# A retention layer whose first two heads take their values by seven products of halves, in turns with queries and keys

## The chip, the core and the metric

The kernel runs on one core of one Trainium2 chip. The metric is the device time of one execution in microseconds (us), the median over runs. Five engines work side by side and meet through semaphores: TensorE (PE in the profile, its weight loads PEld), VectorE (DVE), ScalarE (ACT), GpSimd (POOL) and SyncE (SP), which here only issues DMAs. POOL issues DMAs too: those that add what they bring to what lies in the buffer (accumulate DMAs).

## The reference

Two pre-norm layers on x of 512 tokens by 1024, float32. Layer 0 mixes tokens with a chunked gating MLP, layer 1 with retention; each is followed by a dense MLP with squared ReLU, and a last RMSNorm closes. The change lies in the retention:

```
proj = xn @ w_in                       # xn = rmsnorm(x, g), 1024 wide
q, k, v, g = split(proj)               # 4 heads: q, k 256 wide each; v, g 512 wide each
q = rotary(q, cos, sin); k = rotary(k * dk**-0.5, cos, sin)
o = decayed causal attention of q, k, v   # the kernel: (q k^T * decay) v over all 512 tokens
o = rmsnorm(o per head, head_norm_g) * silu(g)
return o @ w_out
```

## The kernel before

All products are made of 128x512 matmuls on TensorE. Float32 is kept up by splitting every operand in a high part (a rounded copy, made by ACT for weights, `wH`) and a low part (the rest, a subtraction on DVE, `wL`). `mm3` (the matmuls of L265) then issues three matmuls for each product: high by high, high by low, low by high. A piece of weights is 128x1024 or so, and a projection of 1024 inputs to 128 outputs over all tokens is one piece and 24 matmuls; this is one unit of TensorE's work here.

The order of the whole program is written as a list of steps. Each step (`step`) is given its weight pieces. A step issues its matmuls, then `advance` (continues generators that were left pending: second halves of evacuations), then `refill`, which issues the high splits of pieces up to three ahead (`LOOK = 3`) and the low splits up to two ahead, and, when a buffer comes free, the next weight load on SP's queue; then what was hung behind the step. The engines run their own lists in just this order, so what an engine has behind a waiting instruction waits too. Weights land in two buffers of 1 MB of their own (`raw`), and in a third where a stage gives one (`extra`). A generic pool, `bigp`, gives blocks of 1 MB. PSUM has six accumulators (`acc`) and two banks for small things (`mis`).

A layer's norm is applied late: hH and hL hold x times the gain, split, and the factor of each token (`r4` by partition, `rbc` spread over a row) is multiplied in after the product. In retention it goes into the cosines and sines (`trig_scaled`, L869), into the evacuation of v (L906, L907) and of g. The norm's sum of squares is reduced over partitions by two matmuls (`st_mix`, L320, L321) and spread by two (`bc_mix`, L339, L340).

`rope` (L876 to L886) takes the two halves of a head's q or k: four multiplications on DVE, one subtraction and one addition on POOL, then, at the next `advance`, two ACT casts and two DVE subtractions. `scores` makes q k^T by decay, `av` the product with v, `evac_g` the gate, `head_norm` and `make_y` the norm of a head and its split, `o_unit` the output projection. The order is: v of head 0, q and k of head 0, g of head 0 with its scores, q and k of head 1 with `av` of head 0, v of head 1 with its scores and the norm of head 0, g of head 1 with its `av`, output of head 0; then for heads 2 and 3 q and k, v with scores, g with `av`, and the output of the head before.

The dense MLP already uses seven products of halves (Strassen) for its second weight matrix, three times a layer: `seven` (L710 on) splits a product of 512x1024 by 1024x1024 in 256-token, 512-input and 512-output halves. The sums of weights are made by accumulate DMAs on POOL's queue (L200), the sums of activations by `make` (L732 to L755), whose pieces are called `sp`, and the seven products in banks a, b and c are added into `ytok` by ACT (first one, L785) and DVE (L787). There the fourteen pieces of the products take turns with `up` projections.

Of the kernel before, what the change touches and what calls it, by code (L numbers as in the profile page):

```python
# [17 lines left out]
P = 128  # L18
T = 512
# [67 lines left out]
def trunk(ctx, tc, x, norm_mix_g, norm_ffn_g, a_w_in, a_b_in, a_v_norm_g, a_w_s, a_b_s, a_w_out,  # L87
# [6 lines left out]
    bigp = ctx.enter_context(tc.tile_pool(name="bigp", bufs=16))  # L94
# [14 lines left out]

    def z2t(name):  # L110
        return tmp(name, "z2", 4)
# [598 lines left out]
    def seven(l, q):  # L710

        w = mlp_w2[l]

        def part(i, j):
            r, c = 1024 * q + 512 * i, 512 * j
            return w[r : r + 512, c : c + 512].rearrange("(k p) n -> p k n", p=P)
# [6 lines left out]
        lo_t, hi_t = slice(0, T // 2), slice(T // 2, T)  # L723
        sums, parts, banks = {}, {}, {}

        def block(h, ts, c):
            return aF[2 * q + h][:, 2 * c : 2 * c + 2, ts]

        def half(v):
            return v.rearrange("p (k t) -> p k t", t=T // 2)  # L730

        def make(s):  # L732

            def src(c):
                if s in (0, 2, 6):
                    return block(*((0, lo_t), None, (1, lo_t), None, None, None, (1, hi_t))[s], c)
                if s == 1:
                    sums["s", c] = half(tmp(f"sa{l}{q}{c}", "uz"))
                    nc.vector.tensor_sub(out=sums["s", c], in0=block(0, hi_t, c), in1=block(1, hi_t, c))
                elif s == 3:  # L740
                    nc.vector.tensor_sub(out=sums["s", c], in0=sums["s", c], in1=block(0, lo_t, c))
                elif s == 4:
                    nc.vector.tensor_add(out=sums["s", c], in0=sums["s", c], in1=block(1, lo_t, c))
                else:
                    sums["d", c] = half(tmp(f"sd{l}{q}{c}", "sq"))
                    nc.vector.tensor_sub(out=sums["d", c], in0=block(0, lo_t, c), in1=block(0, hi_t, c))
                    return sums["d", c]
                return sums["s", c]

            sp = parts[s] = big([P, 2, 4, T // 2], F32R, f"sp{l}{q}{s}")  # L750
            for c in range(2):
                v = src(c)
                hi, lo = sp[:, 0, 2 * c : 2 * c + 2, :], sp[:, 1, 2 * c : 2 * c + 2, :]
                nc.scalar.copy(out=hi, in_=v)
                nc.vector.tensor_sub(out=lo, in0=v, in1=f32(hi))  # L755
# [5 lines left out]
        PLAN = (0, 1, 2, 3, 5, 4, 6) if q == 2 else range(7)  # L761
# [28 lines left out]

        return (lambda: make(0)), [lambda s=s: [step(one(s, i), pl[s][i]) for i in range(2)] for s in PLAN]

    fresh = set()

    def dense(l, hooks):
# [6 lines left out]
        for q in range(3):  # L802
            pl = pieces_f(mlp_w1[l], (0, D), (1024 * (q + 1), 1024 * (q + 2)))
            first, products = seven(l, q)
# [26 lines left out]
    def down_last(gcol):  # L831
# [14 lines left out]
        for i in range(2, 8):  # L846
            feat(pl[i], last_acts, evac(i), f"dn0_{i}", lambda i=i: back(i))

# [314 lines left out]
```

## Time and profile before

| | |
|---|---|
| time, median of 3 runs | 1373.2 us (1373.09 to 1373.71) |
| the profiled execution's own time | 1372.55 us |
| its span (first to last instruction) | 1370.8 us |
| mean granted TensorE clock | 0.998 |
| PE busy | 1360.1 us (99% of the span) |
| DVE, ACT, POOL busy | 806.8 us (59%), 539.8 us (39%), 164.1 us (12%) |
| retention layer, from its first matmul to its last | 625.55 us to about 1025 us |
| chain of work that ended last | PE 95% |

A row of a group reads: line, engine, operation, output and inputs with their shape, count, then busy time in us, mean duration of one in ns, and the idle time of the engine before them with what ended it. A row of the timeline or of the chain in order of time begins with the start and the duration in us. A row of the table of windows has the length, then each engine's busy time and instruction count, the granted clock, the share of the DMA engines and GB/s.

### The profile page before, as it was taken

What the parts mean: (1) busy time and instruction counts of PE and PEld (TensorE: products, weight loads), DVE (VectorE), ACT (ScalarE), POOL (GpSimd) and SP (SyncE); (2) the same over time, 40 slices, a digit from 0 to 9 for tenths busy, and PEclk for the clock granted to TensorE, in tenths of its full rate; (3) what the DMA queues carried; (4) which work ended last, traced back from release to release, by engine and by line L of the source; (5) the groups of instructions that cost most, each with busy time, mean ns of one, the idle gap of its engine ahead of it and who ended that gap; (6) DMA issues with size and microseconds to landing.
All of it is one profiled execution on the core that took longest, in us unless ns stands there. A gap on an engine that the chain in (4) does not pass through costs nothing.

```text
span 1370.8 us, 15222 instructions
## 1 busy us (share of the span) xinstructions
PE 1360.1 (99%) x6184; PEld 1130.9 (82%) x6184; DVE 806.8 (59%) x1007; ACT 539.8 (39%) x765; POOL 164.1 (12%) x130
## 2 busy tenths in 40 slices
PE   9999999999999999999999999999999999999997
PEld 7888888888888888888888888888888888888886
DVE  7434555675666756775645474365494665665653
ACT  4543423234544434422333432333333543444342
POOL 4001111130100000021112110100121000100002
PEclk9999999999999999999999999999999999999999
DMA  6332222245674848322212222132127375674621
GB/s 234 126 103 92 74 88 87 91 131 154 154 207 126 212 126 183 126 101 95 92 62 75 79 93 93 62 114 71 62 93 212 92 187 159 156 206 127 172 87 61
DMA packets 115798, 166.69 MB, mean 122 GB/s; under 512 B 2880, under 2 KB 67984, under 8 KB 115472
## 3 DMA queue, kind: packets, MB, share of 16 engines
q1 hardware_dynamic: 102448, 139.50, 31.0%
q0 software_dynamic: 12672, 25.17, 10.9%
q8 instruction: 48, 0.79, 0.2%
q10 hardware_dynamic: 608, 1.06, 0.2%
q14 instruction: 22, 0.18, 0.0%
HBM read 163.62 MB, written 2.10 MB: 121 GB/s over the span
## 4 chain that ended last, share of the span: by engine, by line
PE 95%; DVE 2%; DMA 1%; ACT 1%; issue 1%; POOL 0%; SPq 0%; POOLq 0%; ACTq 0%; DVEq 0%
PE up L265 24%; PE g L265 6%; PE ro L265 6%; PE vv L265 6%; PE qk L265 6%; PE u L265 6%; PE o L265 6%; PE v L265 4%; PE dt L265 3%; PE dn L265 2%; PE av L265 2%; PE sm11a L265 2%; PE sm10a L265 2%; PE sm01a L265 2%; PE sm00a L265 2%; PE sm02a L265 2%
## 5 line engine op out<-in xcount | busy, mean ns | idle before, releaser
L228 DVE TENSOR_TENSOR wL<-raw,wH 128x1024 fp32r<-128x1024 f32 x235 | 301.7, 1289 | 63.5 <-PE v L265 18.3
L221 ACT CAST wH<-raw 128x1024 fp32r<-128x1024 f32 x235 | 244.0, 1046 | 86.1 <-PE v L265 15.0
L265 PE MATMUL up<-hH,wH 128*128 128x512 f32 x480 | 187.2, 390 | 0.2 <-ACT xtok L1032 0.2
L265 PE MATMUL up<-hL,wH 128*128 128x512 f32 x480 | 186.8, 389 | 0.0
L265 PE MATMUL up<-hH,wL 128*128 128x512 f32 x480 | 186.8, 389 | 0.0
L687 ACT ACTIVATE aF<-r 128x512 f32<-128x512 f32 x54 | 34.2, 633 | 218.0 <-DVE r L686 218.0
L686 DVE SCALAR_TENSOR_TENSOR r<-up,wide 128x512 f32<-128x512 f32 x54 | 37.4, 692 | 126.5 <-PE up L265 120.1
L265 PEld LDWEIGHTS up<-hH,wH 128*128 128x128 f32 x480 | 90.1, 188 | 19.2 <-ACT xtok L1032 0.5
L265 PEld LDWEIGHTS up<-hH,wL 128*128 128x128 f32 x480 | 90.1, 188 | 18.8
L265 PEld LDWEIGHTS up<-hL,wH 128*128 128x128 f32 x480 | 90.1, 188 | 18.7
L200 POOL DMA_DIRECT2D raw<-in_mlp_w_dram x22 | 28.5, 1297 | 390.4 <-DVE wL L228 244.7
L294 POOL TENSOR_TENSOR ssq<-ssq,sq 128x512 f32<-128x512 f32 x28 | 43.9, 1568 | 151.8 <-ACT sq L293 151.5
L228 DVE TENSOR_TENSOR wL<-more,wH 128x1024 fp32r<-128x1024 f32 x40 | 48.8, 1219 | 5.8 <-issue 4.3
L265 PE MATMUL u<-hH,wH 128*128 128x512 f32 x128 | 50.6, 395 | 0.0
L265 PE MATMUL g<-hH,wH 128*128 128x512 f32 x128 | 50.5, 395 | 0.0
L265 PE MATMUL o<-yH,wH 128*128 128x512 f32 x128 | 50.4, 394 | 0.0
L265 PE MATMUL qk<-hH,wH 128*128 128x512 f32 x128 | 50.0, 391 | 0.0
L265 PE MATMUL vv<-wH,hH 128*128 128x512 f32 x128 | 50.0, 391 | 0.0
L265 PE MATMUL ro<-ryH,wH 128*128 128x512 f32 x128 | 50.0, 390 | 0.0
L265 PE MATMUL ro<-ryH,wL 128*128 128x512 f32 x128 | 50.0, 390 | 0.0
L265 PE MATMUL ro<-ryL,wH 128*128 128x512 f32 x128 | 49.9, 390 | 0.0
L265 PE MATMUL vv<-wL,hH 128*128 128x512 f32 x128 | 49.9, 390 | 0.0
(359 smaller groups left out, 2982.1 us busy)
## 6 DMA issues: line engine op xcount, KB each, us to landing
raw<-in_mlp_w_dram SPq DMA_DIRECT2D x50, 1024.0 KB, 5.1
raw<-in_b_w_in_dram SPq DMA_DIRECT2D x24, 1024.0 KB, 5.0
raw<-in_mlp_w_dram POOLq DMA_DIRECT2D x22, 1024.0 KB, 8.9
more<-in_mlp_w_dram SPq DMA_DIRECT2D x20, 1024.0 KB, 5.2
raw<-in_a_w_in_dram SPq DMA_DIRECT2D x14, 1024.0 KB, 5.2
raw<-in_a_w_out_dram SPq DMA_DIRECT2D x8, 1024.0 KB, 5.0
raw<-in_b_w_out_dram SPq DMA_DIRECT2D x8, 1024.0 KB, 5.0
raw<-in_a_w_in_dram SPq DMA_DIRECT2D x8, 256.0 KB, 6.6
```

The lines of the kernel that those rows point to most:

```text
L200: nc.gpsimd.dma_start(out=r.tile, in_=src, accum_op=ALU.add)
L221: nc.scalar.copy(out=p.hi, in_=p.src)
L228: nc.vector.tensor_sub(out=p.lo, in0=p.src, in1=f32(p.hi))
L265: nc.tensor.matmul(ps, lhsT=a, rhs=b, start=start and i == 0, stop=stop and i == 2, skip_group_check=resumed)
L294: nc.gpsimd.tensor_tensor(out=state["ssq"], in0=state["ssq"], in1=sq, op=ALU.add)
L686: nc.vector.scalar_tensor_tensor(out=r, in0=ps, scalar=0.0, in1=rbc, op0=ALU.max, op1=ALU.mult)
L687: nc.scalar.activation(a, r, AF.Square)
```

## The change

Values of heads 0 and 1 together are a product of 512x1024 by 1024x1024. They are now made by `seven`, as in the dense MLP: seven products of 256-token, 512-input, 512-output halves in place of eight, in the order 0, 1, 2, 3, 5, 4, 6. The activations' side comes from `side_h`: products 0, 2 and 6 use hH and hL as they are, the others use sums built from x times the gain. The results, `vF`, are values without the norm's factor, which is multiplied in when they are split (`split_v`), behind the gates of head 0 and the values of head 2. The pieces of the products take turns with the eight pieces of q and k of heads 0 and 1. The k pieces of these go to the `mis` banks.

With it the order of the layer is rebuilt: after the turns come g of head 0 with its scores, g of head 1 with `av` of head 0, v of head 2 with the scores of head 1 and the norm of head 0, g of head 2 with `av` of head 1, output of head 0, q and k of head 2, output of head 1 with scores of head 2, q and k of head 3 with `av` of head 2, v of head 3, g of head 3, outputs of heads 2 and 3. The evacuation of `av` becomes one DVE instruction for heads 0 to 2. The tables of cosines, sines and decay are loaded at the begin of the layer rather than before the last part of the dense MLP, the decay of two heads at a time; `bigp` has 17 blocks; the third weight buffer of this stage is `morev`; the norm's statistics come after the first product and the first q piece instead of inside v's unit.

```diff
@@ -707,12 +704,12 @@
...
-    def seven(l, q):
-
-        w = mlp_w2[l]
+    def seven(w, row, col, a, dst, name, plan=range(7), behind={}):
...
         def part(i, j):
-            r, c = 1024 * q + 512 * i, 512 * j
+            r, c = row + 512 * i, col + 512 * j
             return w[r : r + 512, c : c + 512].rearrange("(k p) n -> p k n", p=P)
         t1 = Raw(part(0, 0), adds=[part(0, 1)])
...
@@ -720,67 +717,33 @@
...
-            after = dict(zip(PLAN, PLAN[1:])).get(s)
+            then = dict(zip(plan, plan[1:])).get(s)
             def run(p):
                 bk = BANK[s]
                 if i == 0 and s in FIRST:
-                    banks[bk] = [acc(f"sm{l}{q}{bk}{t}") for t in range(2)]
-                sp = parts[s]
+                    banks[bk] = [acc(f"sm{name}{bk}{t}") for t in range(2)]
                 for t in range(2):
-                    ts = slice(t * P, (t + 1) * P)
                     for k in range(2):
                         kk = 2 * i + k
-                        mm3(banks[bk][t], sp[:, 0, kk, ts], sp[:, 1, kk, ts], p.hi[:, k, :], p.lo[:, k, :], s in FIRST and kk == 0, kk == 3, True)
+                        mm3(banks[bk][t], *parts[s](kk, t), p.hi[:, k, :], p.lo[:, k, :], s in FIRST and kk == 0, kk == 3, True)
                 advance()
                 refill()
-                if i == 0 and after is not None:
-                    make(after)
+                if i == 0 and then is not None:
+                    parts[then] = a(then)
+                if (s, i) in behind:
+                    behind[s, i]()
                 if i == 1:
                     (m, n), op = OUT[s]
                     for t in range(2):
-                        v = tok[n][:, 2 * m + t, :]
+                        v = dst[n][:, 2 * m + t, :]
...
@@ -788,7 +751,100 @@
-        return (lambda: make(0)), [lambda s=s: [step(one(s, i), pl[s][i]) for i in range(2)] for s in PLAN]
+        def begin():
+            parts[plan[0]] = a(plan[0])
+        return t1, begin, [lambda s=s: [step(one(s, i), pl[s][i]) for i in range(2)] for s in plan]
...
+    def side_split(sp):
+        return lambda k, t: tuple(sp[:, j, k, t * P : (t + 1) * P] for j in range(2))
...
+    def side_h(gcol, name):
+        sums = {}
+        def g(k):
+            return gT[:, gcol + k : gcol + k + 1]
+        def scaled(c, k0, ts):
+            t = half(sums["all"][:, 2 + c, :])
+            for i in range(2):
+                k = k0 + 2 * c + i
+                nc.scalar.activation(t[:, i, :], xT[k][:, ts], AF.Copy, scale=g(k))
+            return t
+        def combine(out, c, k0, ts, t):
+            for i in range(2):
+                k = k0 + 2 * c + i
+                nc.vector.scalar_tensor_tensor(out=out[:, i, :], in0=xT[k][:, ts], scalar=g(k), in1=t[:, i, :], op0=ALU.mult, op1=ALU.subtract)
+        def make(s):
+            if s in (0, 2, 6):
+                k0, t0 = ((0, 0), None, (4, 0), None, None, None, (4, 2))[s]
+                return lambda k, t: tuple(v[k0 + k][:, (t0 + t) * P : (t0 + t + 1) * P] for v in (hH, hL))
+            sp = big([P, 2, 4, T // 2], F32R, f"sp{name}{s}")
+            for c in range(2):
+                hi, lo = sp[:, 0, 2 * c : 2 * c + 2, :], sp[:, 1, 2 * c : 2 * c + 2, :]
+                if s == 1:
+                    if c == 0:
+                        sums["all"] = big([P, 4, T], F32, f"sa{name}")
+                    v = half(sums["all"][:, c, :])
+                    combine(v, c, 0, hi_t, scaled(c, 4, hi_t))
+                elif s == 5:
+                    v = scaled(c, 0, hi_t)
+                    combine(v, c, 0, lo_t, v)
+                else:
+                    v = half(sums["all"][:, c, :])
+                    combine(v, c, 0 if s == 3 else 4, lo_t, v)
+                if s == 3:
+                    nc.scalar.activation(hi, v, AF.Copy, scale=-1.0)
+                    nc.vector.scalar_tensor_tensor(out=lo, in0=v, scalar=-1.0, in1=f32(hi), op0=ALU.mult, op1=ALU.subtract)
+                else:
+                    nc.scalar.copy(out=hi, in_=v)
+                    nc.vector.tensor_sub(out=lo, in0=v, in1=f32(hi))
+            return side_split(sp)
+        return make
...
@@ -845,33 +901,53 @@
...
+            if i in ahead:
+                ahead[i]()
...
-    do(lambda: (flush(), load_b()))
-    down_last(MIX + 8)
+    do(flush)
...
     bw = b_w_in[0]
...
+    vF, hooks = {}, {}
+    t1, begin_v, vprod = seven(bw, 0, VW, side_h(MIX + 8, "v"), vF, "v", (0, 1, 2, 3, 5, 4, 6), hooks)
+    down_last(MIX + 8, {4: lambda: raws.append(t1)})
...
     def load_b():
-        tab["t"] = big([P, 4, T], F32, "trg")
-        nc.sync.dma_start(out=tab["t"][:, 0:2, :], in_=trig)
-        tab["d"] = big([P, H, T], F32, "dec")
-        nc.sync.dma_start(out=tab["d"], in_=decay)
+        tab["t"] = big([P, 4, T], F32, "tab")
+        tab["raw"] = [zt(f"trg{i}") for i in range(2)]
+        for i in range(2):
+            nc.sync.dma_start(out=tab["raw"][i], in_=trig[:, i, :])
+        load_decay(0)
...
+    def load_decay(h):
+        nc.sync.dma_start(out=tab["t"][:, 2:4, :], in_=decay[:, h : h + 2, :])
     def trig_scaled():
         for i in range(2):
-            nc.vector.tensor_mul(tab["t"][:, 2 + i, :], tab["t"][:, i, :], rbc)
+            nc.vector.tensor_mul(tab["t"][:, i, :], tab["raw"][i], rbc)
...
+    def split_v(h, ns):
+        if 0 in ns:
+            vv[h] = [big([P, NT, DV], F32R, f"vv{n}{h}") for n in "HL"]
+        for n in ns:
+            hi, lo, v = vv[h][0][:, n, :], vv[h][1][:, n, :], vF[h][:, n, :]
+            nc.scalar.activation(hi, v, AF.Copy, scale=r4[:, n : n + 1])
+            nc.vector.scalar_tensor_tensor(out=lo, in0=v, scalar=r4[:, n : n + 1], in1=f32(hi), op0=ALU.mult, op1=ALU.subtract)
     def rope(h, which, pa, pb):
-        cos, sin = tab["t"][:, 2, :], tab["t"][:, 3, :]
+        cos, sin = tab["t"][:, 0, :], tab["t"][:, 1, :]
         if which == 0:
             qk[h] = (big([P, 4, T], F32R, f"qkH{h}"), big([P, 4, T], F32R, f"qkL{h}"))
+        while "tab" not in state:
+            yield
         m = [zt(f"m{h}{which}{i}") for i in range(4)]
         nc.vector.tensor_mul(m[0], pa, cos)
         nc.vector.tensor_mul(m[3], pa, sin)
...
@@ -896,7 +972,13 @@
                 got.append(ps)
                 return rope(h, which, *got) if len(got) == 2 else iter(())
             for i in range(2):
-                feat(pl[i], hs, evac, f"qk{h}{which}{i}", behind.get(2 * which + i))
+                n = 2 * which + i
+                out.append(lambda p=pl[i], evac=evac, n=n, bank=(acc, banks)[which]: feat(p, hs, evac, f"qk{h}{n}", behind.get(n), bank))
+        return out
+
+    def qk_unit(h, behind={}):
+        for p in qk_pieces(h, behind):
+            p()
     def evac_vv(h):
         def ev(n, ps):
...
@@ -949,7 +1031,11 @@
...
-            nc.scalar.activation(o, ps, AF.Copy, scale=gT[:, HG + 4 * h + c : HG + 4 * h + c + 1])
+            gain = gT[:, HG + 4 * h + c : HG + 4 * h + c + 1]
+            if h < 3:
+                nc.vector.scalar_tensor_tensor(out=o, in0=ps, scalar=gain, in1=o, op0=ALU.mult, op1=ALU.mult)
+                return
+            nc.scalar.activation(o, ps, AF.Copy, scale=gain)
...
             nc.vector.tensor_mul(o, o, gt[h][:, c, :])
...
@@ -1005,21 +1091,52 @@
...
-    v_unit(0, {0: nxt(nrm1), 1: nxt(nrm1, 2), 3: nxt(nrm1)})
-    do(trig_scaled)
-    qk_unit(0)
-    g_unit(0, each(scores, 0))
-    qk_unit(1, each(av, 0))
-    hn0, sc1 = head_norm(0), each(scores, 1)
-    fin = {0: nxt(hn0), 1: nxt(hn0, 2), 2: lambda: (next(hn0, None), make_y(0, (0, 1))), 3: lambda: make_y(0, (2, 3))}
-    v_unit(1, {i: (lambda i=i: (sc1[i](), fin[i]())) for i in range(4)})
-    g_unit(1, each(av, 1))
+    def both(*fns):
+        return lambda: [f() for f in fns]
...
+    def with_scores(h, of):
...
+        hn, sc = head_norm(of), each(scores, h)
+        fin = {0: nxt(hn), 1: nxt(hn, 2), 2: both(nxt(hn), lambda: make_y(of, (0, 1))), 3: lambda: make_y(of, (2, 3))}
+        return {i: both(sc[i], fin[i]) for i in range(4)}
...
+    def begin_values():
+        extra.append(big([P, 2048], F32, "morev"))
+        fresh.update((n, m) for n in range(2) for m in range(2))
+        for n in range(2):
+            vF[n] = big([P, NT, DV], F32, f"vF{n}")
+        load_b()
+        begin_v()
...
+    def norm_ready():
+        next(nrm1, None)
+        trig_scaled()
+        state["tab"] = True
...
+    hooks.update({(0, 0): nxt(nrm1), (1, 0): norm_ready})
+    do(begin_values)
+    turns = qk_pieces(0, {0: nxt(nrm1, 2)}, mis) + qk_pieces(1, {}, mis)
+    vprod[0]()
+    turns[0]()
+    for p, t in zip(vprod[1:], turns[1:]):
+        t()
+        p()
+    turns[7]()
+    do(lambda: extra.clear())
+    sc = each(scores, 0)
+    g_unit(0, {0: sc[0], 1: both(sc[1], lambda: split_v(0, (0, 1))), 2: both(sc[2], lambda: split_v(0, (2, 3))), 3: sc[3]})
+    g_unit(1, each(av, 0))
+    vs = with_scores(1, 0)
+    v_unit(2, {0: vs[0], 1: both(vs[1], lambda: split_v(1, (0, 1))), 2: both(lambda: split_v(1, (2, 3)), vs[2]), 3: vs[3]})
+    do(lambda: load_decay(2))
+    g_unit(2, each(av, 1))
     o_unit(0, behind=finish_head(1))
-    for h in (2, 3):
-        qk_unit(h)
-        v_unit(h, each(scores, h))
-        g_unit(h, each(av, h))
-        o_unit(h - 1, behind=finish_head(h))
+    qk_unit(2)
+    o_unit(1, behind=each(scores, 2))
+    qk_unit(3, each(av, 2))
+    v_unit(3, with_scores(3, 2))
+    g_unit(3, each(av, 3))
+    o_unit(2, behind=finish_head(3))
     o_unit(H - 1, gcol=FFN + 8)
```

On DVE at the first q and k of a head, before (`m` are the four products of rope, `qkL` the low splits, wL138 and wL139 the low splits of the pieces of the next head's or the next k's projection):

```order
L876 TENSOR_TENSOR m000_4701<-qk000_4639,trg_4141 128x512
L877 TENSOR_TENSOR m003_4704<-qk000_4639,trg_4141 128x512
L878 TENSOR_TENSOR m001_4702<-qk001_4668,trg_4141 128x512
L879 TENSOR_TENSOR m002_4703<-qk001_4668,trg_4141 128x512
L886 TENSOR_TENSOR qkL0_4700<-m000_4701,qkH0_4699 128x512
L886 TENSOR_TENSOR qkL0_4700<-m002_4703,qkH0_4699 128x512
L228 TENSOR_TENSOR wL138_4694<-raw69_4621,wH138_4693 128x1024
L228 TENSOR_TENSOR wL139_4741<-raw69_4621,wH139_4740 128x1024
```

In the changed kernel, at the k of head 0 (vF0 takes product 2, wL141 is the last piece of product 3, wL142 the piece of head 1's first q, `sav` and `spv5` are the sums for product 5, the fifth):

```order
L750 TENSOR_TENSOR vF0_4482<-vF0_4482,smvb0_4712 128x512
L750 TENSOR_TENSOR vF0_4482<-vF0_4482,smvb1_4713 128x512
L225 TENSOR_TENSOR wL141_4754<-raw64_4043,wH141_4753 128x1024
L952 TENSOR_TENSOR m010_4788<-qk02_4677,tab_4484 128x512
L953 TENSOR_TENSOR m013_4791<-qk02_4677,tab_4484 128x512
L954 TENSOR_TENSOR m011_4789<-qk03_4759,tab_4484 128x512
L955 TENSOR_TENSOR m012_4790<-qk03_4759,tab_4484 128x512
L962 TENSOR_TENSOR qkL0_4624<-m010_4788,qkH0_4623 128x512
L962 TENSOR_TENSOR qkL0_4624<-m012_4790,qkH0_4623 128x512
L225 TENSOR_TENSOR wL142_4785<-raw71_4621,wH142_4784 128x1024
L819 SCALAR_TENSOR_TENSOR sav_4510<-xT0_86,gT_76,sav_4510 128x256 x2
L845 TENSOR_TENSOR spv5_4818<-sav_4510,spv5_4818 128x512
```

The low split that the next projection needs, wL142, stands behind the whole of rope, as wL138 did; additions into vF now stand ahead of rope, and sums for the next product behind.

On ACT around the fifth product (wH143 and wH144 are its weights, wH145 those of head 1's second q; `smva` is the bank that the product before left in, and that the fifth takes next):

```order
L218 CAST wH142_4784<-raw71_4621 128x1024
L961 CAST qkH0_4623<-m010_4788 128x512
L961 CAST qkH0_4623<-m012_4790 128x512
L218 CAST wH143_4814<-morev_4481 128x1024
L812 ACTIVATE sav_4510<-xT0_86,gT_76 128x256 x2
L844 CAST spv5_4818<-sav_4510 128x512
L812 ACTIVATE sav_4510<-xT0_86,gT_76 128x256 x2
L844 CAST spv5_4818<-sav_4510 128x512
L218 CAST wH144_4843<-morev_4481 128x1024
L748 ACTIVATE vF1_4483<-smva0_4490 128x512
L748 ACTIVATE vF1_4483<-smva1_4491 128x512
L218 CAST wH145_4874<-raw71_4621 128x1024
L218 CAST wH146_4892<-raw73_4730 128x1024
```

The copies of smva into vF1, which free the bank, stand behind the casts of the fifth product's weights and sums; in the kernel before, at this place in the layer, ACT had:

```order
L221 CAST wH139_4740<-raw69_4621 128x1024
L221 CAST wH140_4769<-raw70_4697 128x1024
L885 CAST qkH0_4699<-m010_4775 128x512
L885 CAST qkH0_4699<-m012_4777 128x512
L221 CAST wH141_4814<-raw70_4697 128x1024
```

POOL's list, which now has accumulate DMAs between the two instructions of each rope:

```order
L197 DMA raw64_4043<-in_b_w_in_dram 128x4x512
L956 TENSOR_TENSOR m000_4661<-m000_4661,m001_4662 128x512
L957 TENSOR_TENSOR m002_4663<-m002_4663,m003_4664 128x512
L197 DMA morev_4481<-in_b_w_in_dram 128x4x512
L956 TENSOR_TENSOR m010_4788<-m010_4788,m011_4789 128x512
L957 TENSOR_TENSOR m012_4790<-m012_4790,m013_4791 128x512
L197 DMA raw64_4043<-in_b_w_in_dram 128x4x512
```

The second accumulation into raw64 and the one into morev stand behind rope's two instructions and are reached only when these are done.

More of the change, by code (lines that the diff above doesn't have):

```diff
@@ L722, in seven @@
         pl = [[Piece(r, (slice(None), slice(2 * i, 2 * i + 2), slice(None)), [P, 2, 512]) for i in range(2)] for r in wraws]
[L723 to L755, printed above, removed]
+        parts, banks = {}, {}
         BANK = "acbacaa"
@@ new lines, in side_acts, with block, src @@
+    def side_acts(b, name):
+        sums = {}
+        def block(h, ts, c):
+            return aF[b + h][:, 2 * c : 2 * c + 2, ts]
+        def src(s, c):
+            if s in (0, 2, 6):
+                return block(*((0, lo_t), None, (1, lo_t), None, None, None, (1, hi_t))[s], c)
+            if s == 1:
+                sums["s", c] = half(tmp(f"sa{name}{c}", "uz"))
+                nc.vector.tensor_sub(out=sums["s", c], in0=block(0, hi_t, c), in1=block(1, hi_t, c))
+            elif s == 3:
+                nc.vector.tensor_sub(out=sums["s", c], in0=sums["s", c], in1=block(0, lo_t, c))
+            elif s == 4:
+                nc.vector.tensor_add(out=sums["s", c], in0=sums["s", c], in1=block(1, lo_t, c))
+            else:
+                sums["d", c] = half(tmp(f"sd{name}{c}", "sq"))
+                nc.vector.tensor_sub(out=sums["d", c], in0=block(0, lo_t, c), in1=block(0, hi_t, c))
+                return sums["d", c]
+            return sums["s", c]
+        def make(s):
+            sp = big([P, 2, 4, T // 2], F32R, f"sp{name}{s}")
+            for c in range(2):
+                v = src(s, c)
+                hi, lo = sp[:, 0, 2 * c : 2 * c + 2, :], sp[:, 1, 2 * c : 2 * c + 2, :]
[3 more added lines that the diff above has]
+        return make
@@ new lines, in side_h, with make @@
+    def side_h(gcol, name):
+        sums = {}
+        def g(k):
[10 more added lines that the diff above has]
+                nc.vector.scalar_tensor_tensor(out=out[:, i, :], in0=xT[k][:, ts], scalar=g(k), in1=t[:, i, :], op0=ALU.mult, op1=ALU.subtract)
+        def make(s):
+            if s in (0, 2, 6):
+                k0, t0 = ((0, 0), None, (4, 0), None, None, None, (4, 2))[s]
+                return lambda k, t: tuple(v[k0 + k][:, (t0 + t) * P : (t0 + t + 1) * P] for v in (hH, hL))
+            sp = big([P, 2, 4, T // 2], F32R, f"sp{name}{s}")
+            for c in range(2):
+                hi, lo = sp[:, 0, 2 * c : 2 * c + 2, :], sp[:, 1, 2 * c : 2 * c + 2, :]
+                if s == 1:
+                    if c == 0:
[11 more added lines that the diff above has]
+                    nc.vector.scalar_tensor_tensor(out=lo, in0=v, scalar=-1.0, in1=f32(hi), op0=ALU.mult, op1=ALU.subtract)
+                else:
+                    nc.scalar.copy(out=hi, in_=v)
+                    nc.vector.tensor_sub(out=lo, in0=v, in1=f32(hi))
+            return side_split(sp)
+        return make
@@ L803, in dense @@
             pl = pieces_f(mlp_w1[l], (0, D), (1024 * (q + 1), 1024 * (q + 2)))
-            first, products = seven(l, q)
+            _, first, products = seven(mlp_w2[l], 1024 * q, 0, side_acts(2 * q, f"{l}{q}"), tok, f"{l}{q}", (0, 1, 2, 3, 5, 4, 6) if q == 2 else range(7))
             do(first)
@@ L829, in tok0, with down_last @@
         fresh.update((n, m) for n in range(2) for m in range(2))
-    def down_last(gcol):
+    def down_last(gcol, ahead):
         pl = pieces_f(mlp_w2[0], (3072, 4096), (0, D))
@@ L886, in rope, with qk_pieces @@
             nc.vector.tensor_sub(out=lo, in0=mm, in1=f32(hi))
-    def qk_unit(h, behind=None):
-        behind = behind or {}
+    def qk_pieces(h, behind, banks=acc):
+        out = []
         for which in range(2):
@@ L933, in av @@
         if c == 0:
-            oo[h] = big([P, 4, T], F32, f"o{h}")
+            oo[h] = gt[h] if h < 3 else big([P, 4, T], F32, f"o{h}")
         vhi, vlo = vv[h]
@@ L1051, in finish @@
         rsqrt(y, a, 1)
-        o = [zt(f"out0{n}"), z2t(f"out1{n}")]
+        o = [zt(f"out{i}{n}") for i in range(2)]
         nc.vector.scalar_tensor_tensor(out=o[1], in0=tok[1][:, n, :], scalar=y, in1=wide[:, 512:D], op0=ALU.mult, op1=ALU.mult)
```

10 lines of the change are left out of this document (5 added, 5 removed).

## The prediction

> **What bounds the kernel now.** I read the page first, its busy times and the chain that ended last, then the table of windows for the stretches that the change touches, then groups and the timeline. The page says that TensorE is the bound nearly everywhere:
>
> ```profile
> span 1370.8 us, 15222 instructions
> PE 1360.1 (99%) x6184; PEld 1130.9 (82%) x6184; DVE 806.8 (59%) x1007; ACT 539.8 (39%) x765; POOL 164.1 (12%) x130
> ```
>
> The table of windows shows it for three stretches: a dense one where products of halves take turns with `up` projections, the first 99.7 us of retention, and all of retention with the end of the dense part before it.
>
> ```profile
> 338.21:419.81 81.60, 81.60 (x362) 67.57 (x361) 48.59 (x58) 38.40 (x52) 5.16 (x4) 1.00 0.66 168
> 625.55:725.25 99.70, 99.70 (x461) 83.53 (x461) 52.73 (x69) 32.83 (x45) 14.83 (x11) 1.00 0.29 95
> 578.05:1025.35 447.30, 447.30 (x2070) 374.42 (x2069) 262.41 (x346) 150.07 (x216) 68.03 (x50) 1.00 0.26 86
> ```
>
> In each, PE is busy for the whole length at a granted clock of 1.00: retention has no wait to remove, and a matmul that is left out is worth its full length as long as no wait takes its place. The chain in order of time gives the length:
>
> ```profile
> 338.21 5.44 PE sm00a L265 x24
> 343.65 5.44 PE up L265 x24
> ...
> 625.55 10.94 PE vv L265 x48
> 636.49 0.24 PE st_mix L320
> 636.73 0.24 PE st_mix L321
> 636.97 10.93 PE vv L265 x48
> 647.90 0.24 PE bc_mix L339
> 648.14 0.24 PE bc_mix L340
> 648.38 21.81 PE qk L265 x96
> ```
>
> 24 matmuls take 5.44 us, so one takes 0.2267 us, a product of halves as much as a projection.
>
> **What is removed.** Values of heads 0 and 1 take 8 units of 24 matmuls in the order before (v of one head is the two rows of 48 `vv`, 96, and of two heads 192). Seven products take 7 units, 168. All other matmuls stay. The gain is 24 x 0.2267 = **5.44 us**, if nothing waits.
>
> **What the turns ask of the other engines.** 15 units (7 products, 8 pieces of q and k) and the four norm matmuls take 81.6 + 1.0 = 82.6 us on PE. The first window above is the same mix, 7 products and 8 `up` units in 81.60 us, with DVE at 48.6 us (60%) and ACT at 38.4 (47%), and no wait. The turns have more on DVE. Durations are from these groups:
>
> ```profile
> L228 DVE TENSOR_TENSOR wL<-more,wH 128x1024 fp32r<-128x1024 f32 x40 | 48.8, 1219 | 5.8 <-issue 4.3 <-PE sm00a L265 1.5
> L755 DVE TENSOR_TENSOR sp<-sa,sp 128x512 fp32r<-128x512 f32 x36 | 24.9, 692 | 24.7 <-ACT sp L754 24.7
> L886 DVE TENSOR_TENSOR qkL<-m,qkH 128x512 fp32r<-128x512 f32 x16 | 14.4, 902 | 18.0 <-ACT qkH L885 16.9
> L878 DVE TENSOR_TENSOR m<-qk,trg 128x512 f32<-128x512 f32 x8 | 5.5, 692 | 24.1 <-PE qk L265 24.1
> L925 DVE TENSOR_TENSOR pm<-sc,dec 128x256 f32<-128x256 f32 x4 | 1.7, 425 | 10.3 <-PE sc L265 10.3
> L787 DVE TENSOR_TENSOR ytok<-ytok,sm00b 128x512 f32<-128x512 f32 x2 | 1.3, 678 | 0.0
> L324 DVE TENSOR_TENSOR own_mix<-st_mix,ident 128x512 f32<-128x512 f32 x2 | 1.4, 684 | 4.2 <-PE st_mix L321 4.2
> ```
>
> 22 low splits of weights x 1.22 = 26.8; 16 rope multiplications x 0.69 = 11.0; 8 `qkL` x 0.90 = 7.2; 16 scaled sums of 128x256, for which the trace has no such form, at the 0.425 of the nearest, `pm`: 6.8; their 8 low parts x 0.69 = 5.5; 6 additions into vF x 0.68 = 4.1; the two scaled tables and the norm 4.5. Together 66 us, 80% of the stretch. That fits, but DVE runs its list in order, and the second extract of its order above shows weights behind rope. So I followed the list against PE's, place by place.
>
> **Where it will wait.** The first place is the low split wL142 for the first piece of head 1, behind rope of head 0's k. Before, the same work reads, from the end of a head's second piece of qk (648.38 + 10.88 = 659.26):
>
> ```profile
> 655.74 0.68 DVE L876 TENSOR_TENSOR m<-qk,trg 128x512 f32<-128x512 f32 x1
> 656.34 0.68 DVE L877 TENSOR_TENSOR m<-qk,trg 128x512 f32<-128x512 f32 x1
> 659.34 0.69 DVE L878 TENSOR_TENSOR m<-qk,trg 128x512 f32<-128x512 f32 x1 [2.33 <-PE qk L265]
> 659.95 0.68 DVE L879 TENSOR_TENSOR m<-qk,trg 128x512 f32<-128x512 f32 x1
> 660.12 1.29 POOL L880 TENSOR_TENSOR m<-m,m 128x512 f32<-128x512 f32 x1 [20.39 <-DVE m L878]
> 661.36 1.30 POOL L881 TENSOR_TENSOR m<-m,m 128x512 f32<-128x512 f32 x1
> 661.44 0.62 ACT L885 CAST qkH<-m 128x512 fp32r<-128x512 f32 x1 [6.67 <-POOL m L880]
> 662.10 1.94 DVE L886 TENSOR_TENSOR qkL<-m,qkH 128x512 fp32r<-128x512 f32 x2 [1.46 <-ACT qkH L885]
> 663.95 2.35 DVE L228 TENSOR_TENSOR wL<-raw,wH 128x1024 fp32r<-128x1024 f32 x2
> ```
>
> The first of the two wL is done at 663.95 + 1.18 = 665.13, 5.87 us after the piece. In the turns one product (5.44) lies between, and the next piece's first two matmuls need only its high part (2 x 0.227): due at 5.89. With both early multiplications done ahead, as at 655.74 here, the wait is 0; with DVE late and all four behind, it is 2 x 0.61 = 1.2. DVE's work from the norm's spread to the end of head 0's k (one half product, qk02, a product, qk03: 2.72 + 3 x 5.44 = 19.04 us) adds up to 18.4: the copy of the factor 0.65, tables and four multiplications 3.6, five low splits 5.9, lengthening beside POOL 1.1, two `qkL` 1.3, four sums 1.7, two low parts 1.4 with 1.4 of waits for their casts, two additions into vF 1.3; the waits in rope add about 0.6. It arrives just as qk03 ends. I take **+1.0** (0 to 1.2). The same pattern returns at head 1's k with less ahead of it: **+0.35** (0 to 1.2).
>
> The fifth product waits for its bank: the two copies of smva into vF1 stand on ACT behind wH143, the sums for product 5 and wH144. Behind wL142 the sums take four scaled instructions, two casts, two low parts, some 5.8 us with their crossings between ACT and DVE, and the copies 1.3; the fifth product may start about 11.7 to 12.3 after qk03's end, and PE wants it at 10.88, or at 11.9 with the 1.0 above. **+0.2** (0 to 0.4). At the begin, the norm's first split on POOL (a low part at 630.18 before, below) and the third low split have to be done one unit earlier than they were: **+0.2** (0 to 0.5).
>
> Behind the turns I find none. The evacuation of `av` loses one of these two for each of twelve pieces:
>
> ```profile
> L952 ACT ACTIVATE o<-av,gT 128x512 f32<-128x512 f32 x16 | 10.9, 682 | 0.0
> L955 DVE TENSOR_TENSOR o<-o,gt 128x512 f32<-128x512 f32 x16 | 14.1, 879 | 0.0
> ```
>
> That only eases ACT. The splits of vF lie behind gates, whose own DVE work is one instruction a unit, and rope of heads 2 and 3 has a whole output unit behind it. The cover is DVE at 53% in the second window; without it each instruction would cost its own 0.7. I take 0 (0 to 0.5).
>
> Sum: -5.44 + 1.0 + 0.35 + 0.2 + 0.2 = **-3.7 us**. The span goes from 1370.8 to 1367.1, the profiled execution from 1372.55 to 1368.9. The median of the runs stood 0.65 above that execution, so the prediction is **1369.5 us**. With every wait at its low end, 1367.8; at the high ends (3.8 us) 1371.6; the likely case's own range is 1368.3 to 1370.8.
>
> **Rivals.** *No wait at all* (chance 0.13): 1373.2 - 5.4 = 1367.8. For it speaks the first window, where the same turns run without one; against it the order of DVE, which has rope in place of the one `r` instruction of `up`.
>
> *The sum of weights for the fifth product lands late* (0.25). Its base is loaded by SP into `morev`, once wL138 has freed that, and then POOL's accumulate DMA adds the other part. By the durations of such issues:
>
> ```profile
> raw<-in_b_w_in_dram SPq DMA_DIRECT2D x24, 1024.0 KB, 5.0
> raw<-in_mlp_w_dram POOLq DMA_DIRECT2D x22, 1024.0 KB, 8.9
> ...
> DMA to landing us min/median/max: 8.4/8.9/12.6
> ```
>
> The last of these rows is from the view of the line that issues the accumulations. wL138 ends some 10 us after the spread, so the sum is there at 10 + 5.0 + 8.9 = 23.9, and ACT comes to wH143 at about 24.1: nothing is left over. Landing at 12.6, the longest seen, moves wH143, the sums behind it and the copies by 3.5 and with them PE, since the bank has no slack either: -3.7 + 3.5 = -0.2, about 1373.0. That POOL must first finish rope's two instructions (the last extract of the order) works the same way. Against it: 8.9 is the median. What POOL and DVE do to each other shows at the norm before:
>
> ```profile
> 627.86 1.59 POOL L294 TENSOR_TENSOR ssq<-ssq,sq 128x512 f32<-128x512 f32 x1 [4.35 <-ACT sq L293]
> 628.22 2.32 DVE L228 TENSOR_TENSOR wL<-raw,wH 128x1024 fp32r<-128x1024 f32 x1
> 630.18 1.51 POOL L312 TENSOR_TENSOR st_mix<-ssq,st_mix 128x512 fp32r<-128x512 f32 x1 [0.73 <-ACT st_mix L311]
> ```
>
> A low split takes 2.32 us beside an addition on POOL, 1.22 alone. The Trainium skill, "SBUF — State Buffer", section "SBUF: two separate sides", puts this down to a port pair that one of the two engines holds for a whole instruction, and warns that transfers issued from GpSimd wait for their descriptors in the same way while VectorE holds it. By that rule the accumulations land later here, where VectorE is 80% busy, than the 8.9 of a stretch at 60%, and this rival would be the likeliest; the trace of before has no accumulation beside a VectorE as busy as that, so it shows neither. The skill's "TensorE: Matmul & The Clock Gate", section "Part 1: The HAM clock gate", adds that an idle time of about 3.4 us halves the clock for a while; no idle time in the three windows is near that, and the granted clock is 1.00 in all.
>
> *VectorE becomes the bound of the turns* (0.20), slower than before. Its list is then one chain with all its own waits: 66 busy; four ropes with the idle time in front of `qkL` (18.0 in the group for eight ropes: 9.0); eight low parts behind their casts, 24.7/36 each: 5.5; the norm's 4.2; lengthening beside POOL, 8 rope instructions and three accumulations that POOL holds 1.28 us each, 1.1 us of loss in half of them: 6. Together 91. Before, this work took PE 82.6 + 5.44 = 88.0; so from 88.0 on the change loses, and at 91 the time is 1373.2 + 3 = 1376. For it speaks that DVE is held by rope at each second unit; against it that most of these waits overlap the slack of 20% and that a low split is asked for two units ahead.
>
> **How the numbers follow.** The forecast has 0.42, the others 0.13, 0.25 and 0.20. A measurement of this kernel tells about 0.2%, 2.7 us, from no change, so faster means under 1370.5. Of the forecast's 0.42, 0.38 lies there, and all of no wait; 0.04 and 0.21 of the late sum and 0.03 of the last are within 0.2%; 0.17 of the last and 0.04 of the late sum are slower. Faster 0.51, same 0.28, slower 0.21. The range of 8 in 10 goes from 1367.4, just below no wait, to 1375.4, which leaves out the upper half of the last rival and a little below.
>
> **What would show it.** In the chain of the changed kernel: 15 rows of 24 matmuls of smv and qk, with a DVE row of wL of about 1 us ahead of head 1's first piece, and an ACT row of vF1 ahead of the fifth product. Right if the idle time of PE in the turns is 1 to 3 us and stands there. If PE waits for wH143 and this for the landing of `morev`, the second rival; if waits for wL stand in front of five or more units, the third. DVE should read 66 us busy in the turns, a sum 0.42 each, the accumulations 8.9. Wrong from the ground if retention behind the turns shows waits, which I put at nothing.

## The result

The changed kernel takes 1378.01 us (median of 6 runs, 1377.75 to 1379.21), the kernel before 1373.16 us beside it (6 runs): ratio 1.0037, 95% interval 1.0024 to 1.0050. It is slower by 4.9 us; 3.7 us faster was forecast. The profiled execution of the changed kernel is the longest of its runs, 1379.21 us. Its page gives a span of 1377.5 us, and for the engines:

```profile
PE 1361.0 (99%) x6160; PEld 1128.7 (82%) x6160; DVE 829.5 (60%) x1043; ACT 551.8 (40%) x783; POOL 170.0 (12%) x134
```

The 24 matmuls are gone (6184 became 6160), but TensorE is not less busy. From the first matmul of retention to the first of the dense part behind it the chain has 405.85 us (626.27 to 1032.12), before 399.80 (625.55 to 1025.35): 6.05 more. The rows of the dense part's first matmuls, in the changed kernel and then before:

```profile
1032.12 4.76 PE up10a L262 x21
```

```profile
1025.35 4.76 PE up10a L265 x21
```

Another 0.7 us of the profiled span lies ahead of retention. 399.80 - 5.44 = 394.36 would be retention without a wait, so 11.5 us came in. (By the medians it is 4.9 + 5.4 = 10.3; what follows splits the 11.5 of the profiled execution.) The table of windows of the changed kernel, for the turns and for the gates of head 0 with the first of head 1, shows where most of it is:

```profile
626.27:712.04 85.77, 83.84 (x366) 68.02 (x365) 64.85 (x84) 39.40 (x56) 16.38 (x12) 1.00 0.62 171
712.04:750.25 38.21, 34.26 (x145) 28.09 (x145) 17.46 (x25) 14.17 (x20) 2.54 (x2) 0.91 0.09 29
```

The turns take 85.77 us, 3.2 over the 82.6 of the matmuls. The second stretch has a granted clock of 0.91, the only one of retention below 1.00. Before, the same work (four gates with the scores of head 0, and one unit behind them) stood in the chain between these rows:

```profile
670.19 5.44 PE g L265 x24
...
701.31 1.85 PE av L265 x12
```

701.31 - 670.19 = 31.1 us; here it takes 38.2, **7.1 us more**. The view of TensorE's waits over retention agrees:

```profile
PE g L262 <- DVE wL L225: 3.9, 1, 3.9
PE qk L262 <- DVE wL L225: 1.1, 2, 0.9
PE smva L262 <- ACT vF L748: 0.8, 1, 0.8
PE sc L262 <- DVE qkL L962: 0.4, 1, 0.4
```

(Columns: total, times, longest.) The timeline of TensorE at the long wait, first the matmul that waits, then the next of the slow ones and the first at full speed again:

```profile
742.09 0.79 PE L262 MATMUL g<-hH,wL 128*128 128x512 f32 x1 [3.95 <-DVE wL L225]
742.68 0.63 PE L262 MATMUL g<-hH,wH 128*128 128x512 f32 x1
...
748.23 0.40 PE L262 MATMUL g<-hL,wH 128*128 128x512 f32 x1
```

From 742.09 to 748.23 a matmul begins every 0.43 us, where it is 0.227 elsewhere, for 14 matmuls. That is 3.0 us on top of 3.95, in this execution. What TensorE waited for is seen on the other engines. ACT in the changed kernel:

```profile
725.97 0.51 ACT L1008 CAST pH<-pm 128x384 fp32r<-128x384 f32 x1 [2.86 <-DVE pm L1007]
737.67 1.33 ACT L942 ACTIVATE vvH<-vF,r 128x512 fp32r<-128x512 f32 x2 [11.18 <-PE sc L262]
```

And DVE:

```profile
725.38 0.56 DVE L1007 TENSOR_TENSOR pm<-sc,tab 128x384 f32<-128x384 f32 x1 [3.30 <-PE sc L262]
738.42 1.41 DVE L943 SCALAR_TENSOR_TENSOR vvL<-vF,r,vvH 128x512 fp32r<-128x512 f32 x2 [12.48 <-ACT vvH L942]
739.75 0.68 DVE L1068 TENSOR_TENSOR gz<-g,wide 128x512 f32<-128x512 f32 x1
740.35 0.55 DVE L1010 TENSOR_TENSOR pL<-pm,pH 128x384 fp32r<-128x384 f32 x1
740.82 1.22 DVE L225 TENSOR_TENSOR wL<-morev,wH 128x1024 fp32r<-128x1024 f32 x1
```

The split of vF0 is the first to write vvH0. Neither its data nor ACT is late: vF0 is long done, and ACT sits idle for 11 us. It waits for a score, the last one of head 0, which ends at 737.64. In the program (no view of the profile shows addresses) vvH0 has the same address as qkH0, the high parts of q and k of head 0, and all four scores read those. All 17 blocks are in use at this place: x (2), hH and hL (4), vF0 and vF1, the tables, morev, qkH and qkL of two heads (4), pH and pL, the gate. So the split, which stands behind the second gate piece, cannot begin before the last score behind the fourth. The low part vvL0 waits on DVE for the high part, and behind vvL0 stands wL156, the low split that the first gate piece of head 1 needs.

### The profile page after: what moved, and what is told of

Same layout as the page of the kernel before. It is cut to its first block, busy times and chain, and to the rows that moved or that the text cites. A ratio compares the mean times of both kernels' runs of the same rounds, so it can differ in the third digit from the quotient of the medians.

```text
span 1377.5 us, 15250 instructions
## 1 busy us (share of the span) xinstructions
PE 1361.0 (99%) x6160; PEld 1128.7 (82%) x6160; DVE 829.5 (60%) x1043; ACT 551.8 (40%) x783; POOL 170.0 (12%) x134
## 3 DMA queue, kind: packets, MB, share of 16 engines
q0 software_dynamic: 14784, 29.36, 12.6%
## 4 chain that ended last, share of the span: by engine, by line
PE 90%; DVE 4%; ACT 1%; issue 1%; DMA 1%; POOL 1%; POOLq 0%; ACTq 0%; DVEq 0%
PE up L262 24%; PE g L262 7%; PE u L262 6%; PE o L262 6%; PE ro L262 6%; PE qk L262 5%; PE v L262 4%; PE vv L262 3%; PE dt L262 3%; PE dn L262 2%; PE av L262 2%; PE sm11a L262 2%; PE sm10a L262 2%; PE sm01a L262 2%; PE sm00a L262 2%; PE sm12a L262 2%
## 5 line engine op out<-in xcount | busy, mean ns | idle before, releaser
L262 PE MATMUL g<-hH,wL 128*128 128x512 f32 x128 | 51.2, 400 | 3.9 <-DVE wL L225 3.9
L262 PE MATMUL qk<-hH,wL 128*128 128x512 f32 x128 | 50.1, 391 | 1.1 <-DVE wL L225 1.1
L262 PE MATMUL g<-hL,wH 128*128 128x512 f32 x128 | 50.9, 398 | 0.0
```

The source lines that it names most:

```text
L262: nc.tensor.matmul(ps, lhsT=a, rhs=b, start=start and i == 0, stop=stop and i == 2, skip_group_check=resumed)
```

## The experiments

Each is compared with the kernel before, measured beside it (1372.86 to 1373.11 us). The changed kernel was measured only in the result above, beside 1373.16, so a difference to it is known to about 0.3 us.

| edit | median us | ratio to before, 95% interval |
|---|---|---|
| scores_early | 1371.38 | 0.9987 (0.9978 to 0.9996) |
| splits_later | 1372.44 | 0.9996 (0.9987 to 1.0006) |
| keep_busy | 1375.54 | 1.0019 (1.0010 to 1.0029) |
| keep_busy_half | 1376.12 | 1.0022 (1.0013 to 1.0032) |
| no_fifth_sum | 1376.88 | 1.0028 (1.0018 to 1.0038) |
| rope_halves_later | 1369.32 | 0.9973 (0.9962 to 0.9984) |
| scores3_later | 1368.57 | 0.9967 (0.9955 to 0.9980) |
| av_step_later | 1368.13 | 0.9965 (0.9951 to 0.9978) |
| both_later | 1368.31 | 0.9965 (0.9953 to 0.9978) |

**Is it the block, or too much work?** Two edits move what stands around the split.

```diff
-    g_unit(0, {0: sc[0], 1: both(sc[1], lambda: split_v(0, (0, 1))), 2: both(sc[2], lambda: split_v(0, (2, 3))), 3: sc[3]})
+    g_unit(0, {0: both(sc[0], sc[1]), 1: both(sc[2], sc[3]), 2: lambda: split_v(0, (0, 1)), 3: lambda: split_v(0, (2, 3))})
```

> Edit: the four scores of head 0 stand behind the first two gate pieces of head 0, two and two, and the splits of vF0 behind the third and fourth piece. Block theory: vvH0 lies in the block of qkH0 (the same address) and can't be written before the last score of head 0 has read it; in the changed kernel ACT waits 11.2 us for it, DVE behind it 12.5 us, and TensorE 3.95 us for the low split of weights behind that, after which it runs 14 matmuls at 0.43 instead of 0.227 us. With the scores two units earlier the block is free by the time of the split: no wait in the gate of head 1, the stretch of 38.2 us becomes 31.1, the time 1378.0 - 7.1 = 1370.9. Load theory (the splits, gates and scores are too much for ACT and DVE here): at least 2 us of the wait stays in the gates, and the time is above 1375.

1371.38, 6.6 us less than the changed kernel. In the chain of this run the third and fourth gate of head 0 and the first of head 1 are one piece without a gap, 72 matmuls in 16.38 us:

```profile
711.29 5.44 PE g L262 x24
716.73 2.42 PE sc L262 x12
719.15 5.48 PE g L262 x24
724.63 1.33 PE sc L262 x12
725.97 16.38 PE g L262 x72
```

711.29 to 742.35 is 31.06 us, as was expected of the block theory; the load theory, which put at least 2 us of wait here, falls. But this edit moves two things, since the splits too stand one gate piece later than in the changed kernel. The next one moves the splits alone:

```diff
-    g_unit(0, {0: sc[0], 1: both(sc[1], lambda: split_v(0, (0, 1))), 2: both(sc[2], lambda: split_v(0, (2, 3))), 3: sc[3]})
+    g_unit(0, {0: sc[0], 1: sc[1], 2: both(sc[2], lambda: split_v(0, (0, 1))), 3: both(sc[3], lambda: split_v(0, (2, 3)))})
```

> Edit: the scores stay, the two splits of vF0 stand one gate piece later (behind the third and fourth). The block is as late as in the changed kernel. Block theory: vvH0 still begins when the last score ends, but the low split of weights for the gate of head 1 now stands ahead of vvL0 on DVE, so TensorE's 3.95 us and the slow clock behind them go; av of head 0 may wait 0 to 1 us for the second half of the split. Time 1371 to 1372, as far as the list's order and not the work is at fault. Load theory: the wait moves to av of head 0 or to the next gate piece with 3 us or more, time above 1375.

1372.44. The block is still late: the split begins just behind the last score, as at 737.67 in the changed kernel.

```profile
736.71 0.64 PE sc L262 x6
...
737.37 0.73 ACT vvH L942
```

But what is behind it is no longer urgent. The waits of TensorE in this run:

```profile
PE qk L262 <- DVE wL L225: 1.1, 2, 0.9
PE smva L262 <- ACT vF L748: 1.1, 1, 1.1
PE av L262 <- DVE pL L1010: 0.6, 1, 0.6
PE sc L262 <- DVE qkL L962: 0.4, 1, 0.4
```

The 3.9 for wL is gone, and av waits 0.6, within the 0 to 1 that was expected. By the order of events the harm took both: a block that frees late, and a list that put an urgent low split behind the instruction that needs it. In both edits the splits stand later, and no run frees the block earlier and leaves the splits where they were. That the split waits for the last score and not for work of its own is seen in the traces, where it starts 0.02 us behind that score in both places (and at 728.40 in scores_early, with no wait for a score). A version that gives vvH0 another block at the same place in the list was not run, so that this wait is one for the block rests on the address and on the order of events, not on an edit of the block alone.

**Is it the idle time that slows the clock?** Matmuls that nobody reads were put into the idle time.

```diff
+    def keep_warm():
+        ps = acc("warm0")
+        for i in range(16):
+            nc.tensor.matmul(ps, lhsT=hH[0][:, 0:P], rhs=hH[1], start=True, stop=True, skip_group_check=True)
...
-    ... 3: sc[3]})
+    ... 3: both(sc[3], keep_warm)})
```

> Edit: the changed kernel, with 16 matmuls whose result nobody reads behind the last score of head 0, where TensorE idles; they fill 3.6 of its 3.95 us. The wait for the low split stays, and the gate piece behind it begins as late as before. If the idle time is what halves the clock: granted clock 1.00 through the gate piece, its 22 matmuls in 5.0 instead of 8.16 us, time 1378.0 - 3.0 = 1375.0. If the clock falls for another reason (what ACT and DVE draw at that moment), the time stays at 1378.0.

1375.54, against 1375.0 expected. The low split comes as late, at 740.08 in the chain, 28.87 us behind the first gate (28.86 in the changed kernel), and the gate piece behind it runs at full speed:

```profile
740.08 1.15 DVE wL L225
741.26 5.32 PE g L262 x22
```

22 matmuls in 5.32 us, 8.16 in the changed kernel. It is the idle time: the work of ACT and DVE at that moment is the same. How much the clock costs is not fixed, though. In the profile of no_fifth_sum (below) the same idle time of 3.95 us is followed by 11 slow matmuls, not 14:

```profile
741.02 7.47 PE g L262 x22
```

So the two profiles give 2.3 and 3.0 us. The other runs of these two kernels have mean granted clocks of 0.996 to 0.998, where the runs without such an idle time have 0.998 or 0.999, so it probably differs from one execution to the next.

> Edit: as keep_busy with 8 matmuls instead of 16, so that 2.1 of the 3.95 us stay idle. If the clock falls only behind an idle time beyond some length between 2.1 and 3.95: granted clock 1.00 in the gate piece, time as keep_busy, 1375.5. If the loss grows with the idle time: about half of it, 1376.7.

With 8 such matmuls some 2.1 us stay idle. The window around it, the gates and the next piece (columns as in the tables above):

```profile
711.00:760.00 49.00, 46.90 (x221) 39.24 (x220) 22.44 (x31) 18.45 (x26) 3.85 (x3) 1.00 0.15 50
```

The granted clock is 1.00, and the 22 matmuls take 5.30 us: an idle time of 2.1 us costs itself and the slower start of one matmul (0.1), one of 3.95 costs 2.3 to 3.0 more. The time, 1376.12, is 0.6 above keep_busy and 0.6 below what half the loss would give; its runs (1375.36 to 1377.11) overlap those of keep_busy (1375.01 to 1376.24), and its profile holds 1.0 us of wait at the fifth product that the profile of keep_busy lacks. The trace decides this one, not the time. The runs bound the limit between 2.1 and 3.95 us. This agrees with the Trainium skill, "TensorE: Matmul & The Clock Gate", section "Part 1: The HAM clock gate", which puts it at about 3.4 us.

**The turns.** The three waits there, as the timeline of the changed kernel has them:

```profile
672.27 0.50 PE L262 MATMUL qk<-hH,wL 128*128 128x512 f32 x1 [0.90 <-DVE wL L225]
678.37 0.49 PE L262 MATMUL smva<-wH,spv 128*128 128x512 f32 x1 [0.81 <-ACT vF L748]
695.87 0.50 PE L262 MATMUL qk<-hH,wL 128*128 128x512 f32 x1 [0.22 <-DVE wL L225]
```

With the slower start behind each (the next one or two matmuls begin 0.33 to 0.42 apart) they cost 1.2, 1.3 and 0.5 us by the distance from one matmul's start to the next. For the second, the chain on ACT begins with a landing:

```profile
671.68 1.05 ACT L218 CAST wH<-morev 128x1024 fp32r<-128x1024 f32 x1 [1.32 <-DMA morev<-in_b_w_in_dram]
```

That is the accumulation into the weights of the fifth product, which took 9.6 us from issue to landing here. Without it:

```diff
-        ..., Raw(part(0, 1), adds=[part(1, 1)]), t4]
+        ..., Raw(part(0, 1), adds=[] if name == "v" else [part(1, 1)]), t4]
```

> Edit: the changed kernel without the accumulation into the weights of the fifth product (the other part of the sum is left out, so values of heads 0 and 1 are not the reference's). TensorE's wait at the fifth product was 0.8 to 1.05 us in three profiles where that sum landed 9.6 to 9.8 us after its issue, and none in two where it landed after 9.0 and 9.1. If the landing decides: ACT finds the weights there (base load about 5 us after its issue), no wait at the fifth product, while the 0.9 at head 1's first piece and the 3.95 in the gate stay; time 1378.0 - 1.2 = 1376.8. Rival, that the sums of activations and the copies of smva on ACT set it alone: 0.8 stays, 1378.0.

1376.88, and the waits of TensorE in this run lack the row of smva:

```profile
PE g L262 <- DVE wL L225: 4.0, 1, 4.0
PE qk L262 <- DVE wL L225: 1.1, 2, 0.9
PE sc L262 <- DVE qkL L962: 0.4, 1, 0.4
```

So the landing decides: with rope where the changed kernel has it, the profiles with landings of 9.6 to 9.8 had 0.8 to 1.1 us of wait, those with 9.0 and 9.1 none. In all nine profiles with the sum, the fifth product begins 6.7 us behind the start of ACT's cast of these weights. That the landing makes part of the spread from run to run is likely, but only profiles of different kernels show it.

For the other two, rope's second half was moved behind the weights:

```diff
         yield
+        if h < 2:
+            yield
+            yield
+            yield
         for i, mm in ((0, m[0]), (1, m[2])):
```

> Edit: as scores_early, and for heads 0 and 1 the second half of rope (two ACT casts, two low splits on DVE) three steps later, behind the weights of the next product and projection. In the changed kernel the turns have three waits of TensorE, at head 1's first piece (0.9), at the fifth product (0.8) and at head 1's k (0.2), with the slower start behind each 2.9 us of the 3.15 that the turns take over 82.6. Order theory: all three come from rope's second half ahead of weights, the fifth product's through the buffer of its weight sum, which frees later; they go, the turns take 83, and the time is 1378.0 - 7.1 - 2.9 = 1368.0. VectorE theory (its work, 80% of the turns, is the bound): the waits come back at other pieces, the turns take 85 or more, and the time is 1370.5 or more.

1369.32. The turns, from 625.69 to 708.85, take 83.16 us, 0.6 over the matmuls, and the window of this run shows TensorE busy throughout, while DVE does more in it than in the same window of the changed kernel (64.85):

```profile
626.00:711.00 85.00, 85.00 (x374) 69.71 (x373) 68.17 (x87) 40.27 (x57) 19.67 (x14) 1.00 0.62 173
```

The order was at fault, not VectorE's load, which falls as a theory: 68.2 us of work in 85 without a wait. The fifth product's sum is issued 2 us earlier (659.79 for 661.97), since the low splits that free its buffer no longer stand behind rope. The time is 1.3 above the 1368.0 expected; what was missing lies behind the gates.

**What is left.** In the chain of the changed kernel the norm of head 1 goes over seven steps before TensorE gets its statistics (st_h) in the output of head 0:

```profile
830.47 0.61 ACT sqh L1032
...
831.11 0.75 DVE gt L1036
831.86 0.61 DVE gz L1068
...
832.49 0.63 ACT gt L1069
833.12 0.94 ACT wH L218
834.06 0.53 ACT st_h L308
...
834.65 1.53 POOL st_h L309
...
836.22 0.50 PE st_h L318
```

`gt` at L1036 is the merged instruction that takes av out. It stands ahead of the gate's gz on DVE, and ACT's silu, weight cast and statistics cast follow gz. At head 3 the same instruction stands ahead of rope, and the first score waits. Two edits on top of rope_halves_later, alone and together:

```diff
-    v_unit(3, with_scores(3, 2))
+    hn3, sc3 = head_norm(2), each(scores, 3)
+    v_unit(3, {0: nxt(hn3), 1: both(sc3[0], nxt(hn3, 2)), 2: both(sc3[1], sc3[2], nxt(hn3), lambda: make_y(2, (0, 1))), 3: both(sc3[3], lambda: make_y(2, (2, 3)))})
```

> Edit: as rope_halves_later, and in the values of head 3 the scores of that head one piece later (0, 1, 2 and 1 behind the four pieces). In all kernels of the new order the first score of head 3 stands one unit behind the k of its head and waits 0.4 us for the low split of that k, since av of head 2 puts its own instruction ahead of rope on DVE; the unit of values takes 27.5 us there and 26.55 in the kernel before. If rope is late for this score, the wait goes: 1369.3 - 1.0 = 1368.3. Rival, that the unit is long because of the norm of head 2 in it (statistics behind av): no change, 1369.3.

```diff
             if h < 3:
+                yield
                 nc.vector.scalar_tensor_tensor(out=o, in0=ps, scalar=gain, in1=o, op0=ALU.mult, op1=ALU.mult)
```

> Edit: as rope_halves_later, and the one DVE instruction that takes av out for heads 0 to 2 stands one step later. In the chain, the statistics of head 1's norm wait at the output of head 0: from the last av over ACT's square, the DVE instruction of av, the gate's gz, its silu, a weight cast, the statistics' cast and POOL to the matmul of the statistics, 0.35 us after TensorE wanted it. If it is the merged instruction ahead of gz that makes it late, the output of head 0 gets 0.5 us shorter: 1369.3 - 0.5 = 1368.8. Rival, that POOL's low part sets it whatever stands ahead: 1369.3.

> Edit: the edits of scores3_later and av_step_later together. If the two waits are all that is left: 1369.3 - 1.5 = 1367.8, which is the time before less the 24 matmuls (1373.2 - 5.4); if the waits only move, 1368.8 to 1369.3.

1368.57, 1368.13 and 1368.31; the three can't be told apart by the times. By the chains, retention takes 396.29 us in rope_halves_later, and 395.29, 395.07 and 395.26 here. By the chains the first edit gave the 1.0 expected. The second gave 1.2 where 0.5 was expected, since it also takes the merged instruction from ahead of rope in head 3: no score waits in its profile either. Together they give no more: the second edit alone removes both waits, which had one cause, and my expectation counted it twice. These versions beat both kernels; av_step_later, with the smaller of the two edits, is 4.9 us faster than the kernel before. In it 0.7 us over 394.36 is left, and its only wait of TensorE in retention stands again at the fifth product, whose sum landed after 9.3 us there:

```profile
PE smva L262 <- ACT vF L748: 0.2, 1, 0.2
```

With the slower start behind it, that product and the piece of queries and keys ahead of it take 11.64 us instead of 10.88.

## Why the prediction was wrong

Wrong was the step "Behind the turns I find none ... I take 0 (0 to 0.5)". It measured 8.4 us: 7.1 in the gates and about 1.3 at the norm of head 1 and the scores of head 3 (11.5 less the 3.15 of the turns and the 7.1). Its reasons failed one by one.

- "The splits of vF lie behind gates, whose own DVE work is one instruction a unit" looked at the load of the engine and not at where the split's output goes. The change's own text said that the pool has 17 blocks; a count of those in use at the split gives 17, and the one that vvH0 gets is read by the scores behind it. The wait was in neither the range nor a rival.
- "Rope of heads 2 and 3 has a whole output unit behind it" holds for head 2. Head 3's q and k are followed by its values with the first score behind one piece of 5.44 us, and av of head 2 is in between.
- "That only eases ACT", of the merged instruction: it waits for ACT's square (831.08 in the chain) and holds DVE's list, which an instruction on ACT with its product two steps later did not.

The clock was weighed and left aside: "no idle time in the three windows is near that". That was true of before, and the sum had no wait long enough. Where a wait is a fault of order and can be of any length, the limit belongs to its price: 3.95 us cost 7.0 in the profiled execution.

By the other steps, from the profiled execution:

- The gain of 5.44: right. Retention without waits is 394.36, and av_step_later comes within 0.7 of it.
- The turns, predicted 82.6 + 1.75, took 85.77, so 3.15. Head 1's first piece: +1.0 predicted, 0.90 of idle time and 1.2 with the slow start behind it. Head 1's k: +0.35, measured 0.22, with the start 0.5. The fifth product: +0.2 predicted, 0.81 and 1.3 measured in this execution, none in those where the sum landed at 9.0. The begin: +0.2, measured none. The places were right; the start behind each wait, 0.3 to 0.5 us, was left out.
- DVE's 66 us in the turns: 64.85. A scaled sum, estimated at 0.425 by the mean of the nearest group, took 0.478 by its own mean; two of them in a row overlap and take 0.87.
- The rival of the late sum was real, with 1.3 us where 3.5 was priced: landings of 9.0 to 9.8 us in nine profiles, not 12.6. The Trainium skill, "SBUF — State Buffer", section "SBUF: two separate sides", warns that a transfer issued from GpSimd waits for its descriptors while VectorE holds their shared ports. By that rule this would have been the likeliest way to lose. The traces don't bear it out in general: with VectorE busy 64.85 of 85.77 us, the fifth product's sum landed 0.1 to 0.9 later than the 8.9 of the dense part, but the two other sums issued in the turns landed after 8.2 to 8.8 us in the nine profiles. Another candidate is a load on SP's queue, issued at 657.42 and landing 6.5 us later in the changed kernel, which was still on its way when the fifth sum was issued at 661.97. What delays that sum was not tested.
- VectorE as the bound: wrong, by rope_halves_later.
- The sign of slower had a chance of 0.21, but from other causes than the one that acted.

## What to carry to other kernels

When a change lengthens lives, count the blocks of each pool at every allocation, and ask for a new tile whose place it takes, who reads that last, and what stands behind the instruction that will wait: this reads as an engine idle for long behind a result that is not its input. A low split or cast that the bound engine needs next goes ahead of work that is not urgent, and half of rope could wait three steps at no cost here. An idle time of the bound engine is not priced by its length alone once it comes near the length that lowers its clock.

## What the runs showed of the hardware

After 3.95 us without a matmul TensorE ran 14 matmuls at 0.43 us each instead of 0.227, about 6 us, and then at full speed again; after the same 3.95 us in no_fifth_sum it ran 11 so, 4.8 us. After 2.1 us (keep_busy_half) it ran none. Behind shorter waits, of 0.2 to 0.9 us, the granted clock stays at 1.00, and still the next one or two matmuls begin 0.33 to 0.42 us apart, so that in the turns a short wait cost 0.3 to 0.5 us more than its length.
